# One pool for attention's tiles over the row sums, sample columns by ScalarE, adaptive weights in row tiles, bias by GpSimd

## The chip, the cores and the metric

The kernel runs on one core of a Trainium2 chip. The metric is the device time of one execution in microseconds (us). The engines are named as in the profile: PE is TensorE (matmuls; PEld is its weight load), DVE is VectorE, ACT is ScalarE, POOL is GpSimd, SP is SyncE, which here only issues transfers. Matmuls read from on-chip memory (SBUF) and write into banks of the accumulator memory (PSUM).

## The reference

One layer of a streaming encoder runs on two groups of requests that share the weights: a prompt of 1024 tokens and a sample of 32 tokens with a cache of 512 past tokens. Width 1024, eight heads of 64. Cut to what matters here:

```
ada = silu(c) @ w_ada + b_ada            # 6 vectors of 1024: shift, scale, gate, twice
h   = rms_norm(x) * (1 + scale1) + shift1
p   = h @ w_in                           # q-latent, kv-latent, rope key, q, k, v of branch B, two gates
o_A = latent attention (softmax)         # branch A
o_B: z = q k^T / 8;  sp = softplus(z) under a strict causal mask
     a = exp(log_sigmoid(z) - sum of sp over later keys);  o_B = a @ v     # branch B, stick-breaking
x   = x + gate1 * rms_norm((sigmoid(g_a) * (o_A @ w_proj_a) + sigmoid(g_b) * (o_B @ w_proj_b)) @ w_out)
x   = x + gate2 * rms_norm(conv_ffn(...))
```

Of the six vectors of ada the first two are needed before h; the other four (v = 2 to 5) are computed beside branch B's attention. All data is 32-bit floating point.

## The kernel before

Matmuls run in a reduced 32-bit format. For accuracy each operand is split into a high part (ScalarE, `hi`, L65) and a low part (VectorE, `lo`, L68), and each product is three matmuls (`mm3`, L72 to L74). Tokens are 1024 + 32 = 1056 columns; weights come in tiles of 128 by 1024.

The stages run one after the other: `stage_h` (norm, 0 to some 50 us), `stage_qkv` (projections to q, k, v), `stage_sb` (branch B's attention together with the gate projections and the rest of ada), `stage_lat` and `stage_mla` (branch A), then merge and feed-forward. The change lies in `stage_qkv` and `stage_sb` and at the border between them.

**`stage_qkv`.** The first q and k tile and a latent tile are plain products. The other ten tiles go in five pairs (`pair`) with a Strassen-like scheme: sums of quarters of h (pool "sums": T4, T3, T1, T2, two buffers each of 8448 bytes a partition, in this order of addresses) are multiplied with sums of quarters of the weights (`half`; the weights' sums are made by DVE in L585 to L590, partly in tile S1). S1 is the first 1024 columns of S0, the buffer in which the first k tile was projected. The results land in quarters of `fq` (U) as tiles of [128, 1056]. `after` then handles each finished tile: q is scaled and split, k is split, k and v are also transposed to natural order (`natural`, L466 and L472) and stored as outputs; all parts that attention needs are spilled to DRAM ("qh", "ql", "kh", "kl", "vd") by POOL's queue (L459, L478, L485). The last 32 columns of each tile, the sample's, go into one tile `sb` by a small copy on POOL (L487, L496, L504); it is stored to DRAM at the end of the stage (L665). The high part of the last two q tiles is kept in T1[0] until it is stored.

**`stage_sb`.** Four passes p, each for two heads (h = 0, 1). The order of the instructions of PE, ACT and DVE within a pass is written out by hand in `ORDER`: S is a score product, a, e, l, x, c, d, E are the steps from a score to weights, T a transpose, h and v the split of the transposed weights, V the product with the values, o and p the sum of two parts (L768, L770). Each score block has a row tile "A" (five buffers of 4096 bytes), and a score bank ("s", three) that is free again after step d (L739). "f" advances a generator, `gates().steps`: per tile m of the gate projection two adaptive steps (`ada_step`: a weight tile of 128 by 1024 from `w_ada`, eight matmuls, L216), then 24 steps of three gate matmuls. The adaptive weight tiles share the two buffers "wr" of pool W with the weight tiles of the projections. Eight adaptive steps make one vector v; its sum with the bias (L226) goes into the tile "ada" (one buffer), which the four bias transfers (L224) fill before. For v = 2 and 5 the result is stored from there (L248).

SP's queue issues the loads in the order that the planner finds: queries (L1087, six transfers of 256 KB a head), values (L1083, 512 KB), adaptive weights (L214), gate weights (L82), bias (L224). A transfer waits on the queue until its buffer is free, and all behind it wait too. The planner may move an instruction without dependencies far ahead of its place in the program, also into the hand-written order. The sample's attention (`sb_sample`) is written behind the four passes; two of its instructions stand early in the profile: the memset of QZ (L965) and the loads of cached values (L974).

**Memory.** There is a left and a right stack. On the left, above the constants and pool W, lie `fq` and the pool "qkv"; on the right, below the tiles of h, lies "sums". At the border, `att_pools` allocates the pool "att" on the left, where `fq` and "qkv" were: rows A, the transposed weights PTh and PTl, o, nat, big, QZ. `stage_sb` allocates the pool "sb" on the right over "sums": V, KL, Q and KH of both heads, reset, ptd, ada. A new tile waits for the readers of those old tiles that lay at its addresses.

Of the kernel before, what the change touches and what calls it, by code (L numbers as in the profile page):

```python
# [8 lines left out]
F32 = mybir.dt.float32  # L9
# [8 lines left out]
P = 128  # L18
D = 1024
# [25 lines left out]
class K:  # L45
# [8 lines left out]

    BUFS = {"A": 5, "Q": 3, "big": 3, "o": 2, "QZ": 1, "t": 5, "mh": 4, "ml": 4, "dh": 3, "dl": 3, "ada": 1, "G": 1, "Gs": 1, "xs": 1, "jk": 1, "s": 3, "pv": 1, "tr": 2, "mm": 2, "KSm": 1, "VSm": 1, "ObH": 1, "ObL": 1, "sg": 2}

# [149 lines left out]
    def ada_step(self, n, pool, tp, late):  # L206
# [4 lines left out]
        for i, (v, k) in enumerate(self.ada_todo[:n]):  # L211
            w = self.tl(pool, [P, D], F32, "wr")
            with self.tc.issue_after(self.begun):
                nc.sync.dma_start(w, a["w_ada"][0, k * P : (k + 1) * P, v * D : (v + 1) * D])  # L214
            for j in range(4):
                nc.tensor.matmul(ps[32 * j : 32 * j + 32, :256], self.cT[:, k], w[:, j * 256 : j * 256 + 256],  # L216
                                 start=i == 0, stop=i == n - 1)
            if i < n - 1:
                yield
        if self.ada_todo[0][1] == 0:  # L220
            self.acc = self.tl(tp, [P, 256], F32, "ada")
            for j in range(4):
                c = v * D + j * 256
                nc.sync.dma_start(self.acc[32 * j : 32 * j + 32], a["b_ada"][0, c : c + 256].partition_broadcast(32))  # L224
        acc = self.acc
# [199 lines left out]
    def stage_qkv(self):  # L425
# [35 lines left out]
        def natural(u, p, name, t0):  # L461
# [17 lines left out]
            if name == "v":  # L479
# [6 lines left out]
                else:  # L486
                    nc.gpsimd.tensor_copy(self.vsb[:, p * P : p * P + P], st[:r, :P])  # L487

        def after(kind, p, u):
# [3 lines left out]
            if kind == "q":  # L493
                QH = sg() if p == 1 else flat(T1[0])[:, TP * (p - 2) : TP * (p - 1)]
                self.hi(QH, x, 0.125)
                nc.gpsimd.tensor_scalar(self.qsb[:, p], u[:, TP:T], 0.125, None, ALU.mult)  # L496
                spill("qh", p, QH)
                stt(low, x, 0.125, fl(QH), ALU.mult, ALU.subtract)
                spill("ql", p, low)
                return  # L500
            if kind == "k":
                KH = sg()
                self.hi(KH, x)
                nc.gpsimd.tensor_copy(self.ksb[:, p], u[:, TP:T])  # L504
                spill("kh", p, KH)
# [239 lines left out]
    def sums(self, V, out, tiles):  # L745
# [3 lines left out]
        def do(k, x, h, u):  # L749
# [14 lines left out]
            else:  # L764
# [4 lines left out]
                else:  # L769
                    nc.vector.tensor_tensor(res[n][r], pv[n][r, :256], res[n][r], ALU.add)  # L770
                    out(res[n], r, slice(u * 256, u * 256 + 256))
# [188 lines left out]
    def sb_sample(self, b):  # L960
# [3 lines left out]
        QZ = self.tl(self.sm2, [P, 4, 64], F32, "QZ")  # L964
        nc.vector.memset(QZ, 0.0)  # L965
        for h in range(2):
# [3 lines left out]
        ck = self.tl(self.At, [P, TP], F32, "A")  # L970
        nc.sync.dma_start(ck.rearrange("p (t c) -> p t c", t=4),
                          a["cache_sb_k"][0, 0, :, hs].rearrange("(t p) h d -> p t (h d)", p=P))
        cv = self.tl(self.At, [P, BIG], F32, "big")
        nc.sync.dma_start(cv[:, :TP].rearrange("p (t c) -> p t c", t=4),  # L974
                          a["cache_sb_v"][0, 0, :, hs].rearrange("(t p) h d -> p t (h d)", p=P))
# [79 lines left out]

    def att_pools(self):
        nc = self.nc
        self.sm2 = self.At = self.tc.alloc_tile_pool(name="att", bufs=2, reuse_waits="tile")
        for g, w, n in (("o", 256, 2), ("big", BIG, 3), ("QZ", 256, 1), ("nat", 512, 2)):
            for _ in range(n):  # L1060
                self.tl(self.At, [P, w], F32, g)
        self.obd, self.oad = ([self.dr.tile([P, T], F32, name=f"{n}{k}") for k in range(4)] for n in ("ob", "oa"))
# [11 lines left out]
    def stage_sb(self):  # L1074
        nc = self.nc
        S = self.Sp = self.tc.alloc_tile_pool(name="sb", bufs=1, side="right", reuse_waits="tile")
        self.KLz, Q, KH, V = [None] * 2, [None] * 2, [None] * 2, [None] * 2
        t = lambda n: self.tl(S, [P, TP], F32R, n)

        def values(p, h):  # L1080
            if p:
                V[h] = t(f"V{h}")
            nc.sync.dma_start(V[h].bitcast(F32).rearrange("r (t d) -> r t d", t=8), self.vd[p][:, :, h])  # L1083

# [15 lines left out]
        first(1)  # L1100
        self.reset = S.tile([P, 512], BF16, name="reset")
        nc.vector.memset(self.reset, 1.0)
        nc.vector.tensor_scalar(self.reset[:, 383:511], self.idt, -1.0, 1.0, ALU.mult, ALU.add)
        self.diagonals(S)
        first(0)

# [10 lines left out]
        for p in range(4):  # L1117
# [3 lines left out]
            with self.tc.manual_schedule(engines={E.PE, E.Activation, E.DVE}):  # L1121
                self.sb_attend(score, lambda b, h: V[h][:, b * P : b * P + P], self.store(self.obd[p]), fill, then)
        self.in_w.append(self.next_w.pop(0))
        x = self.tl(self.At, [P, TP], F32, "A")
        self.sample_views(x)
# [3 lines left out]
        self.sample_rest = self.sb_sample(1)  # L1129
        self.Sp.release()  # L1130

# [1368 lines left out]
    def run(self, upto=99):  # L2500
        self.consts()
        self.stage_h()
        self.stage_qkv()
        self.att_pools()
        self.stage_sb()
# [60 lines left out]
```

## Time and profile before

| | us |
|---|---|
| median of 3 runs | 1715.2 (1713.25 to 1717.47) |
| the profiled execution | 1714.1 |
| its span | 1712.3 |
| PE busy | 1663.3 (97%) |
| DVE busy | 1274.1 (74%) |
| ACT busy | 991.4 (58%) |
| POOL busy | 297.3 (17%) |
| mean granted clock of PE | 0.99 of full |

The span runs from the first to the last instruction of the profiled execution. Busy times are sums over the span; matmuls are pipelined and their ends are modelled, so a busy PE may still be slow: the granted clock says how fast. An idle time before an instruction carries the name of what ended it; "issue" means that the profile shows no releaser. A transfer's "landing" is the time from its issue to its last byte. Where a row stands for several instructions (x2), its duration runs from the start of the first to the end of the last.

### The profile page before, as it was taken

What the parts mean: (1) busy time and instruction counts of PE and PEld (TensorE: products, weight loads), DVE (VectorE), ACT (ScalarE), POOL (GpSimd) and SP (SyncE); (2) the same over time, 40 slices, a digit from 0 to 9 for tenths busy, and PEclk for the clock granted to TensorE, in tenths of its full rate; (3) what the DMA queues carried; (4) which work ended last, traced back from release to release, by engine and by line L of the source; (5) the groups of instructions that cost most, each with busy time, mean ns of one, the idle gap of its engine ahead of it and who ended that gap; (6) DMA issues with size and microseconds to landing.
All of it is one profiled execution on the core that took longest, in us unless ns stands there. A gap on an engine that the chain in (4) does not pass through costs nothing. (4 is left out here: it accounts for less than half of the span.)

```text
span 1712.3 us, 30291 instructions
## 1 busy us (share of the span) xinstructions
PE 1663.3 (97%) x11646; PEld 1517.1 (89%) x11646; DVE 1274.1 (74%) x2129; ACT 991.4 (58%) x1934; POOL 297.3 (17%) x564
## 2 busy tenths in 40 slices
PE   5999799999999999999999999999999999999997
PEld 3999798998999899988889789999999999977886
DVE  4765496979794588877776779887787787788456
ACT  4544386978784577777773476544444444544442
POOL 3213211111111131111100121221121121110013
PEclk9999899999999999999999999999999999999999
DMA  9335875555633331222174531423333333697643
GB/s 329 100 120 188 277 200 170 161 164 164 175 112 93 118 97 53 65 65 71 58 275 149 182 123 54 151 93 130 130 99 133 132 102 131 233 338 240 224 141 120
DMA packets 185984, 255.19 MB, mean 149 GB/s; under 512 B 14703, under 2 KB 125569, under 8 KB 185841
## 3 DMA queue, kind: packets, MB, share of 16 engines
q1 hardware_dynamic: 165712, 194.63, 36.6%
q0 software_dynamic: 19904, 58.56, 9.7%
q8 instruction: 91, 1.49, 0.4%
q14 instruction: 53, 0.43, 0.1%
q10 hardware_dynamic: 224, 0.09, 0.0%
HBM read 187.86 MB, written 64.57 MB: 147 GB/s over the span
## 5 line engine op out<-in xcount | busy, mean ns | idle before, releaser
L65 ACT ACTIVATE wh<-wr 128x1024 fp32r<-128x1024 f32 (+5 forms) x163 | 132.1, 820 | 224.9 <-PE s L2019 78.6
L68 DVE TENSOR_TENSOR wl<-wr,wh 128x1024 fp32r<-128x1024 f32 (+5 forms) x163 | 151.3, 936 | 84.8 <-ACT wh L65 84.7
L72 PE MATMUL mm<-hh,wh 128*128 128x352 f32 x456 | 155.8, 342 | 0.0
L73 PE MATMUL mm<-hl,wh 128*128 128x352 f32 x456 | 151.1, 331 | 0.4 <-DVE hl L312 0.4
L74 PE MATMUL mm<-hh,wl 128*128 128x352 f32 x456 | 150.5, 330 | 0.0
L2018 PE MATMUL mm<-T,wh 128*128 128x256 f32 (+1 forms) x376 | 108.7, 289 | 2.6 <-ACT q L592 2.6
L2020 PE MATMUL mm<-T,wl 128*128 128x256 f32 (+1 forms) x376 | 107.6, 287 | 0.3 <-DVE wl L68 0.2
L2019 PE MATMUL mm<-T,wh 128*128 128x256 f32 (+1 forms) x376 | 107.3, 286 | 0.0
L2018 PE MATMUL s<-T,wh 128*128 128x256 f32 (+1 forms) x348 | 99.4, 286 | 0.0
L2020 PE MATMUL s<-T,wl 128*128 128x256 f32 (+1 forms) x348 | 99.2, 285 | 0.0
L2019 PE MATMUL s<-T,wh 128*128 128x256 f32 (+1 forms) x348 | 99.1, 285 | 0.0
L68 DVE TENSOR_TENSOR wl<-S,wh 128x1024 fp32r<-128x1024 f32 (+1 forms) x55 | 59.2, 1078 | 47.4 <-ACT wh L65 47.1
L72 PEld LDWEIGHTS mm<-hh,wh 128*128 128x128 f32 x456 | 87.8, 193 | 7.2 <-ACT o L768 3.3
L73 PEld LDWEIGHTS mm<-hl,wh 128*128 128x128 f32 x456 | 88.0, 193 | 2.7 <-DVE hl L312 0.9
L2159 DVE SCALAR_TENSOR_TENSOR u<-u,c,u 128x1058 f32<-128x1058 f32 x68 | 87.0, 1316 | 2.0 <-ACT u L2156 0.7
L74 PEld LDWEIGHTS mm<-hh,wl 128*128 128x128 f32 x456 | 88.0, 193 | 0.4 <-issue 0.3
L782 PE MATMUL tr<-c,A 128*128 128x128 f32 x576 | 84.1, 275 | 1.2 <-ACT A L741 0.6
L65 ACT ACTIVATE wh<-S 128x1024 fp32r<-128x1024 f32 (+1 forms) x55 | 51.8, 943 | 55.1 <-PE s L2019 13.4
L2018 PE MATMUL tr<-T,wh 128*128 128x272 f32 (+1 forms) x272 | 77.7, 286 | 0.0
L2020 PE MATMUL tr<-T,wl 128*128 128x272 f32 (+1 forms) x272 | 77.6, 285 | 0.1
L2019 PE MATMUL tr<-T,wh 128*128 128x272 f32 (+1 forms) x272 | 77.3, 284 | 0.0
L2018 PEld LDWEIGHTS mm<-T,wh 128*128 128x128 f32 x376 | 71.2, 189 | 4.1 <-ACT q L592 2.8
(754 smaller groups left out, 5785.7 us busy)
## 6 DMA issues: line engine op xcount, KB each, us to landing
wr<-in_w_ada_dram SPq DMA_DIRECT2D x48, 512.0 KB, 5.8
wr<-in_w_up_dram SPq DMA_DIRECT2D x44, 512.0 KB, 4.0
dr<-in_w_down_dram SPq DMA_DIRECT2D x43, 512.0 KB, 5.9
wr<-in_w_in_dram SPq DMA_DIRECT2D x33, 512.0 KB, 4.8
wr<-gdn SPq DMA_DIRECT2D x30, 512.0 KB, 4.9
gdn<-u POOLq DMA_DIRECT2D x23, 512.0 KB, 5.3
gd<-nat POOLq DMA_DIRECT2D x48, 176.0 KB, 2.9
t<-gd SPq DMA_DIRECT2D x16, 528.0 KB, 5.8
```

The lines of the kernel that those rows point to most:

```text
L65: self.nc.scalar.activation(out, in_, AF.Identity, scale=scale)
L68: return self.nc.vector.tensor_tensor(out, full, hi.bitcast(F32), ALU.subtract)
L72: m(ps, lh, rh, start=start, stop=False)
L73: m(ps, lh, rl, start=False, stop=False)
L74: self.pe = m(ps, ll, rh, start=False, stop=stop).ins
L782: self.nc.tensor.transpose(tr[:, (2 * s + q) * P : (2 * s + q + 1) * P], at[q][:, b * P : b * P + P], self.idt)
L2018: m(ps[:, :n], w[0][:, k], x[0][:, k, c], start=first and k == 0, stop=False, skip_group_check=True)
L2019: m(ps[:, :n], w[0][:, k], x[1][:, k, c], start=False, stop=False, skip_group_check=True)
L2020: i = m(ps[:, :n], w[1][:, k], x[0][:, k, c], start=False, stop=k == 3, skip_group_check=True)
L2159: nc.vector.scalar_tensor_tensor(y, u[:, w : w + YW], self.cvT[:, w, cc : cc + 1], y, ALU.mult, ALU.add)
```

## The change

- The tiles of branch B's attention (PTh, PTl, o, nat, and the five rows A) move from the left pool into the right pool "sb", which is now 74752 bytes and lies over "sums" and a little below it. By the order of allocation the rows A lie over the end of T3 and over T1, head 0's tiles over the end of T1 and T2, head 1's over T4 and T3, o and nat over T4[0], PTh and PTl below. The left pool "att" is allocated only behind the four passes, for the sample and branch A. `att_pools` becomes `att_rows` (the DRAM tiles alone).
- The high part of the last two q tiles is kept in T4[0], no longer in T1[0].
- The sample's columns are copied by ScalarE; for v straight from the PSUM bank.
- The first two adaptive weight tiles go into two of the rows A (`ada_first`), not into "wr".
- "ada" has two buffers, and the bias is loaded by POOL's queue.
- QZ's memset may only come behind the last sum of the passes (L770), and the loads of cached keys and values only behind the last load of values (L1083).

```diff
--- before.py
+++ after.py
@@ -52,7 +52,7 @@
         self.n += 1
         return f"{s}_{self.n}"
 
-    BUFS = {"A": 5, "Q": 3, "big": 3, "o": 2, "QZ": 1, "t": 5, "mh": 4, "ml": 4, "dh": 3, "dl": 3, "ada": 1, "G": 1, "Gs": 1, "xs": 1, "jk": 1, "s": 3, "pv": 1, "tr": 2, "mm": 2, "KSm": 1, "VSm": 1, "ObH": 1, "ObL": 1, "sg": 2}
+    BUFS = {"A": 5, "Q": 3, "big": 3, "o": 2, "QZ": 1, "t": 5, "mh": 4, "ml": 4, "dh": 3, "dl": 3, "ada": 2, "G": 1, "Gs": 1, "xs": 1, "jk": 1, "s": 3, "pv": 1, "tr": 2, "mm": 2, "KSm": 1, "VSm": 1, "ObH": 1, "ObL": 1, "sg": 2}
 
     def tl(self, pool, shape, dt=F32, tag=None, bufs=None):
         return pool.tile(shape, dt, tag=tag, name=self.nm(tag or "t"), bufs=bufs or self.BUFS.get(tag))
@@ -209,7 +209,7 @@
         nc, a = self.nc, self.a
         ps = self.bank("mm")
         for i, (v, k) in enumerate(self.ada_todo[:n]):
-            w = self.tl(pool, [P, D], F32, "wr")
+            w = self.ada_first.pop(0) if self.ada_first else self.tl(pool, [P, D], F32, "wr")
             with self.tc.issue_after(self.begun):
                 nc.sync.dma_start(w, a["w_ada"][0, k * P : (k + 1) * P, v * D : (v + 1) * D])
             for j in range(4):
@@ -221,7 +221,7 @@
             self.acc = self.tl(tp, [P, 256], F32, "ada")
             for j in range(4):
                 c = v * D + j * 256
-                nc.sync.dma_start(self.acc[32 * j : 32 * j + 32], a["b_ada"][0, c : c + 256].partition_broadcast(32))
+                nc.gpsimd.dma_start(self.acc[32 * j : 32 * j + 32], a["b_ada"][0, c : c + 256].partition_broadcast(32))
         acc = self.acc
         late.append(lambda: nc.vector.tensor_tensor(acc, acc, ps[:, :256], ALU.add))
         del self.ada_todo[:n]
@@ -484,16 +484,16 @@
                     add(V[:, :, :, 64:128], sv, fl(V[:, :, :, 0:64]), ALU.subtract)
                     nc.gpsimd.dma_start(self.vd[p][:, t0 : t0 + 4], fl(V))
                 else:
-                    nc.gpsimd.tensor_copy(self.vsb[:, p * P : p * P + P], st[:r, :P])
+                    nc.scalar.copy(self.vsb[:, p * P : p * P + P], tr[:r, :P])
 
         def after(kind, p, u):
 
             x = u[:, :TP]
             low = x.bitcast(F32R)
             if kind == "q":
-                QH = sg() if p == 1 else flat(T1[0])[:, TP * (p - 2) : TP * (p - 1)]
+                QH = sg() if p == 1 else flat(T4[0])[:, TP * (p - 2) : TP * (p - 1)]
                 self.hi(QH, x, 0.125)
-                nc.gpsimd.tensor_scalar(self.qsb[:, p], u[:, TP:T], 0.125, None, ALU.mult)
+                nc.scalar.mul(self.qsb[:, p], u[:, TP:T], 0.125)
                 spill("qh", p, QH)
                 stt(low, x, 0.125, fl(QH), ALU.mult, ALU.subtract)
                 spill("ql", p, low)
@@ -501,7 +501,7 @@
             if kind == "k":
                 KH = sg()
                 self.hi(KH, x)
-                nc.gpsimd.tensor_copy(self.ksb[:, p], u[:, TP:T])
+                nc.scalar.copy(self.ksb[:, p], u[:, TP:T])
                 spill("kh", p, KH)
             for t0 in (0, 4, 8):
                 natural(u, p, kind, t0)
@@ -767,7 +767,7 @@
                     res[n] = self.tl(self.At, [P, 256], F32, "o")
                     nc.scalar.copy(res[n][r], pv[n][q, :256])
                 else:
-                    nc.vector.tensor_tensor(res[n][r], pv[n][r, :256], res[n][r], ALU.add)
+                    self.sum_ins = nc.vector.tensor_tensor(res[n][r], pv[n][r, :256], res[n][r], ALU.add).ins
                     out(res[n], r, slice(u * 256, u * 256 + 256))
 
         return do
@@ -962,16 +962,19 @@
         nc, a = self.nc, self.a
         os = self.osb
         QZ = self.tl(self.sm2, [P, 4, 64], F32, "QZ")
-        nc.vector.memset(QZ, 0.0)
+        with self.tc.issue_after(self.sum_ins):
+            nc.vector.memset(QZ, 0.0)
         for h in range(2):
             r, pc = slice(64 * h, 64 * h + 64), slice(2 * b, 2 * b + 2)
             nc.vector.tensor_copy(QZ[r, pc, 32 * h : 32 * h + 32], self.qsb[r, pc])
         hs = slice(4 * b, 4 * b + 4)
         ck = self.tl(self.At, [P, TP], F32, "A")
-        nc.sync.dma_start(ck.rearrange("p (t c) -> p t c", t=4),
+        with self.tc.issue_after(self.fetched):
+            nc.sync.dma_start(ck.rearrange("p (t c) -> p t c", t=4),
                           a["cache_sb_k"][0, 0, :, hs].rearrange("(t p) h d -> p t (h d)", p=P))
         cv = self.tl(self.At, [P, BIG], F32, "big")
-        nc.sync.dma_start(cv[:, :TP].rearrange("p (t c) -> p t c", t=4),
+        with self.tc.issue_after(self.fetched):
+            nc.sync.dma_start(cv[:, :TP].rearrange("p (t c) -> p t c", t=4),
                           a["cache_sb_v"][0, 0, :, hs].rearrange("(t p) h d -> p t (h d)", p=P))
         mm = [self.tl(self.At, [P, TP], F32, "A") for _ in range(2)]
         for pp in range(2):
@@ -1053,12 +1056,7 @@
 
         return do
 
-    def att_pools(self):
-        nc = self.nc
-        self.sm2 = self.At = self.tc.alloc_tile_pool(name="att", bufs=2, reuse_waits="tile")
-        for g, w, n in (("o", 256, 2), ("big", BIG, 3), ("QZ", 256, 1), ("nat", 512, 2)):
-            for _ in range(n):
-                self.tl(self.At, [P, w], F32, g)
+    def att_rows(self):
         self.obd, self.oad = ([self.dr.tile([P, T], F32, name=f"{n}{k}") for k in range(4)] for n in ("ob", "oa"))
         self.gd = self.dr.tile([16, P, T], F32, name="gd")
         self.pbd = self.dr.tile([8, P, T], F32, name="pbd")
@@ -1073,14 +1071,18 @@
 
     def stage_sb(self):
         nc = self.nc
-        S = self.Sp = self.tc.alloc_tile_pool(name="sb", bufs=1, side="right", reuse_waits="tile")
+        self.att_rows()
+        S = self.Sp = self.At = self.tc.alloc_tile_pool(name="sb", bufs=2, side="right", reuse_waits="tile")
+        for g, w, n in (("PTh", 512, 2), ("PTl", 512, 2), ("o", 256, 2), ("nat", 512, 2)):
+            for _ in range(n):
+                self.tl(S, [P, w], F32R if g[0] == "P" else F32, g)
         self.KLz, Q, KH, V = [None] * 2, [None] * 2, [None] * 2, [None] * 2
-        t = lambda n: self.tl(S, [P, TP], F32R, n)
+        t = lambda n: self.tl(S, [P, TP], F32R, n, 1)
 
         def values(p, h):
             if p:
                 V[h] = t(f"V{h}")
-            nc.sync.dma_start(V[h].bitcast(F32).rearrange("r (t d) -> r t d", t=8), self.vd[p][:, :, h])
+            self.fetched = nc.sync.dma_start(V[h].bitcast(F32).rearrange("r (t d) -> r t d", t=8), self.vd[p][:, :, h]).ins
 
         def queries(p, h):
             r, o = slice(64 * h, 64 * h + 64), slice(64 - 64 * h, 128 - 64 * h)
@@ -1098,10 +1100,13 @@
             V[h], self.KLz[h], Q[h], KH[h] = t(f"V{h}"), t(f"KL{h}"), t(f"Q{h}"), t(f"KH{h}")
 
         first(1)
-        self.reset = S.tile([P, 512], BF16, name="reset")
+        self.reset = S.tile([P, 512], BF16, name="reset", bufs=1)
         nc.vector.memset(self.reset, 1.0)
         nc.vector.tensor_scalar(self.reset[:, 383:511], self.idt, -1.0, 1.0, ALU.mult, ALU.add)
         self.diagonals(S)
+        self.ada_first = [self.tl(S, [P, D], F32, "A") for _ in range(2)]
+        for _ in range(3):
+            self.tl(S, [P, TP], F32, "A")
         first(0)
 
         self.begun = queries(0, 0)
@@ -1121,13 +1126,14 @@
             with self.tc.manual_schedule(engines={E.PE, E.Activation, E.DVE}):
                 self.sb_attend(score, lambda b, h: V[h][:, b * P : b * P + P], self.store(self.obd[p]), fill, then)
         self.in_w.append(self.next_w.pop(0))
+        S.release()
+        self.sm2 = self.At = self.tc.alloc_tile_pool(name="att", bufs=2, reuse_waits="tile")
         x = self.tl(self.At, [P, TP], F32, "A")
         self.sample_views(x)
         self.osb = x[:, 768:896].rearrange("p (k t) -> p k t", k=4)
         for r, c in self.SB:
             nc.sync.dma_start(x[r, c], self.sbd[r, c])
         self.sample_rest = self.sb_sample(1)
-        self.Sp.release()
 
 
     def lat_sums(self, sq):
@@ -2501,7 +2507,6 @@
         self.consts()
         self.stage_h()
         self.stage_qkv()
-        self.att_pools()
         self.stage_sb()
         self.stage_lat()
         self.stage_mla()
```

## The prediction

> **What bounds the kernel now.** I read the page first: its first part (busy time of each engine) and the rows for PE and DMA of its second (forty equal slices).
>
> ```profile
> span 1712.3 us, 30291 instructions
> PE 1663.3 (97%) x11646; PEld 1517.1 (89%) x11646; DVE 1274.1 (74%) x2129; ACT 991.4 (58%) x1934; POOL 297.3 (17%) x564
> PE   5999799999999999999999999999999999999997
> DMA  9335875555633331222174531423333333697643
> ```
>
> TensorE sets the end: 1712.3 − 1663.3 = 49 us of the span are without a matmul. A gain can come only from those 49 us and from matmuls at a low granted clock. The change touches slices 2 to 13 of 42.8 us each, and the fifth (171 to 214 us) is the poor one: PE at 7 tenths, DMA at 8. So I took busy time by stretch next, around every place in those slices where PE stood. The columns are stretch, length, busy us (instructions) of PE, PEld, DVE, ACT and POOL, then clock, DMA share, GB/s.
>
> ```profile
> 88.00:92.00 4.00, 2.72 (x18) 2.72 (x19) 4.00 (x6) 2.09 (x4) 0.01 (x1) 0.84 0.34 135
> 92.00:96.00 4.00, 4.00 (x26) 4.00 (x26) 4.00 (x6) 2.20 (x5) 0.00 (x0) 0.73 0.52 131
> 195.00:200.00 5.00, 1.73 (x17) 0.95 (x14) 3.74 (x6) 1.31 (x2) 3.11 (x8) 0.99 1.02 409
> 210.00:215.00 5.00, 3.44 (x12) 3.24 (x13) 4.49 (x10) 4.05 (x10) 0.00 (x0) 0.52 1.02 213
> 215.00:220.00 5.00, 5.00 (x29) 5.00 (x28) 3.02 (x8) 3.81 (x9) 0.86 (x2) 0.80 1.06 266
> 288.00:292.00 4.00, 2.28 (x24) 1.14 (x23) 2.42 (x7) 3.55 (x12) 0.55 (x1) 1.00 1.00 326
> 292.00:296.00 4.00, 4.00 (x17) 3.92 (x16) 2.13 (x4) 0.38 (x1) 0.00 (x0) 0.57 0.62 186
> ```
>
> Three places, each an idle PE followed by a low clock: near 87 us (start of the paired projections), 196 to 217 us (from projections to attention), 289 to 296 us (attention's second pass). The change meets all three. Below, rows of the timeline give start, us, engine and line; a bracket gives the idle time before and what ended it.
>
> **1. Sample's columns to ScalarE (L487, L496, L504).** Eleven small copies leave POOL.
>
> ```profile
> 69.02 8.07 POOL L504 COPY sb<-S 128x32 f32<-128x32 f32 x1 [5.78 <-ACT S L649]
> L504 POOL COPY sb<-fq x3: 209/209/211, 128.5 to 150.1; 128x32 f32<-128x32 f32 x3
> 79.08 0.55 POOL L459 DMA_DIRECT2D kl<-S  x1
> DMA to landing us min/median/max: 4.5/4.5/4.5
> 83.62 0.69 DVE L585 TENSOR_TENSOR S<-wr 128x512 f32<-128x512 f32 x1 [6.60 <-issue]
> 89.28 0.39 PE L2018 MATMUL mm<-T,wh 128*128 128x256 f32 x1 [2.58 <-ACT q L592]
> L641 ACT ACTIVATE sb<-mm x1: 198/198/198, 62.4 to 62.4; 128x32 f32<-128x32 f32 x1
> ```
>
> The first of L504 took 8.07 us where the other three took 0.21, and POOL's queue stood behind it until 77.1: the key store kl<-S went out at 79.08, 2.0 us after the copy, and landed 4.5 us later (its landing row), at 83.6. That is when DVE's L585 starts, which overwrites the S that the store still reads. So the 6.60 us of DVE, called "issue", are this store, and DVE was free at 83.62 − 6.60 = 77.0. Without the copy POOL sends its stores as their inputs come; the same chain with 0.2 in place of 8.07 puts kl 7.9 earlier, at 71.2, if its input is there, and a store that waits for its input some 2 us more: 73.7, landing at 78.2. L585 and the ScalarE copies behind it (L592) then come 83.6 − 78.2 = 5.4 us earlier, more than the 2.58 that PE waited for L592, so that wait goes. The low clock behind it cost 4 × (1 − 0.73) = 1.1 in 92 to 96 and up to 4 × (1 − 0.84) = 0.6 before, together some 1.6. Gain 2.6 + 1.6 = 4.2. Late next is PE's own queue: its stretch from 92 on is full.
>
> ScalarE takes the eleven at 0.2 us (L641's row, the same shape): 2.2 us, on an engine busy 2.09 of 4 us here, each behind a ScalarE operation that needs the same input. Bounds: 0, and 2.2 if each lay on PE's path. I take 0.4, nearer to the covered end.
>
> **2. The border to attention.**
>
> ```profile
> 197.90 0.64 PE L216 MATMUL mm<-wr,cT 128*32 128x256 f32 x8 [1.81 <-ACT T L65]
> 201.21 1.08 PE L216 MATMUL mm<-wr,cT 128*32 128x256 f32 x8 [2.67 <-DMA wr<-in_w_ada_dram]
> 206.49 0.46 PE L74 MATMUL mm<-hh,wl 128*128 128x352 f32 x1
> 211.56 0.76 PE L1112 MATMUL s<-KH,Q 128*128 128x512 f32 x1 [4.61 <-DVE A L739]
> 199.67 0.29 DVE L1103 TENSOR_SCALAR reset<-c 128x128 bf16<-128x128 f32 x1
> 209.28 0.27 DVE L965 MEMSET QZ<- 128x256 f32 x1 [9.32 <-DMA ql<-fq]
> 196.78 1.06 ACT L65 ACTIVATE T<-fq 128x1024 fp32r<-128x1024 f32 x1 [1.18 <-DVE fq L576]
> 201.12 0.28 ACT L721 ACTIVATE A<-s 128x128 f32<-128x128 f32 x1 [3.29 <-DMA out_dram<-nat]
> 186.63 7.74 SPq L214 DMA_DIRECT2D wr<-in_w_ada_dram  x2
> ```
>
> PE's 4.61 waits for DVE's L739, which frees the score bank; L739 is late because DVE's queue stood 9.32 us at the memset of QZ. That tile is for the sample's attention, 300 us later; it lies where the projections' buffers were, and their store ql<-fq landed at 209. ScalarE's first L721 waits for such a store in the same way. In the changed kernel the row tiles A lie over T1 and the end of T3, which are read out before the projections end, and the memset is tied behind the last L770. So L721 can run behind the last split of the queries (196.78 + 1.06 = 197.8), five more short ScalarE operations bring DVE's L727 to about 200, where L1103 ends, and L739 frees the bank 211.56 − 209.28 = 2.3 us later, at 202.3. The next step is late instead: the two adaptive loads. They now go out together (before: 186.63 and 7.74 later), but one behind the other on SP's queue, with the DMA at a share of 1.02. So I leave 1.81 and 2.67 as they are; the other bound is that both go, 4.5. PE then comes to its next score at 206.49 + 0.46 = 206.95, and the 4.61 are gone. So is the low clock behind them: (215 − 211.56) × (1 − 0.52) + 5 × (1 − 0.80) = 1.65 + 1.0 = 2.6. I take 2.5. Gain 7.1.
>
> A rule beside that row: the Trainium skill, "TensorE: Matmul & The Clock Gate", Part 1, puts the warm-up at about 3.4 us at half clock, an estimate of 1.7 us lost for each stall. By the rule the term would be 4.6 + 1.7 = 6.3; the rows show more lost here, and the rows decide.
>
> The queries' high part moves from T1 to T4: its two stores (L459) now hold V1 back and no longer Q1. V1 belongs to the second pair of heads, which starts later. Priced 0; what covers it are the first pair's blocks.
>
> **3. Bias by POOL, two buffers.**
>
> ```profile
> SPq L224 <- DMA gtd<-ada: 6.4, 1, 6.4
> 284.12 0.56 SPq L1083 DMA_DIRECT2D V<-vd  x1
> 285.29 0.35 SPq L214 DMA_DIRECT2D wr<-in_w_ada_dram  x1
> 290.90 0.64 PE L216 MATMUL mm<-wr,cT 128*32 128x256 f32 x8 [1.72 <-DMA wr<-in_w_ada_dram]
> 288.62 0.55 POOL L1044 DMA_DIRECT2D gd<-nat  x1 [3.31 <-ACT A L721]
> 299.37 0.54 POOL L1044 DMA_DIRECT2D gd<-nat  x1 [10.20 <-ACT nat L1043]
> 369.99 0.54 POOL L1044 DMA_DIRECT2D gd<-nat  x1 [3.32 <-ACT A L721]
> 377.51 0.54 POOL L1044 DMA_DIRECT2D gd<-nat  x1 [6.98 <-ACT nat L1043]
> 443.58 0.55 SPq L1083 DMA_DIRECT2D V<-vd  x1
> 446.32 0.35 SPq L214 DMA_DIRECT2D wr<-in_w_ada_dram  x1
> ```
>
> SP stood 6.4 us until the one bias buffer was stored. So V left at 284.12, 1.2 us before the adaptive load of 285.29; that load landed at 290.9, and PE wanted it at 290.90 − 1.72 = 289.2. In a pass where nothing held SP, V leaves 2.7 us ahead of that load (443.58, 446.32). The price of the stall with its low clock: from 288.62 to 299.37 lie 10.75 us, between the same two stores one pass later 377.51 − 369.99 = 7.52. That is 3.2; I take 3.0, since a shorter wait may stay. POOL gets sixteen issues of 0.54 us, 8.6 us on an engine 17% busy: 0. Its queue carries only stores here; what waits for the bias is DVE's sum of it, which the order of work places some steps after the issue.
>
> **4. The sample's loads move.**
>
> ```profile
> 224.60 0.38 SPq L974 DMA_DIRECT2D big<-in_cache_sb_v_dram  x1
> DMA to landing us min/median/max: 5.0/5.0/5.0
> DMA to landing us min/median/max: 4.1/4.1/4.1
> ```
>
> Cached keys (L971) and values (L974) may now issue only behind the last V load, 443.58, and the buffers of the keys are free by then. Up to three loads of 512 KB can come in before the adaptive load of 446.32, which has no slack: it lands 4.1 us later (second landing row), at 450.4, when PE wants it. Bounds: 0 if they go behind it, as the value load of before went behind an adaptive load in the first pass; and 3 × 5.0 (the first landing row, of the value loads) = 15 us of stall with 2.5 of low clock, 17.5. I take 0, by the nearest row, 224.60.
>
> **Sum.** 4.2 − 0.4 + 7.1 + 3.0 = 13.9. The profiled execution took 1714.1 (its span 1712.3 and 1.8 around it), 1.1 under the median of 1715.2. 1714.1 − 13.9 = 1700.2; against the median 1701.3.
>
> **The rivals.**
> A. kl<-S is late through traffic and not through POOL, and part 1 gives nothing: 1715.2 − 9.7 = 1705.5. Against it: the store's issue itself is late, right behind the copy.
> B. The bias move gives nothing, since the load of 285.29 is slow through traffic: 1701.3 + 3.0 = 1704.3. For it: a DMA share of 1.00 from 288 to 292. Against it: what held V was a semaphore. The Trainium skill, "DMA: Bandwidth & Descriptors", section "Issuing engines are not separate DMA queues", says that another issuing engine saves only issue time, since all share the same 16 engines; that rule makes B.
> C. Part 4 at a middle price. Three loads at 1.3 us (512 KB at the 409 GB/s of 195 to 200) are 3.9, with 2 of low clock 5.9: 1707.2. At 3.3 each (what the second adaptive load took behind the first, 201.2 − 197.9) 9.9 + 2.5 = 12.4: 1713.7, no change.
> D. The memset goes, but another row tile or store holds DVE or ScalarE about as long, and part 2 gives half or nothing: 1704.9 to 1708.4.
> E. Slower: part 4 at its dear end, 17.5 against 13.9: 1718.8. It decides from 13.9 us on, 3.8 of stall a load with the clock. For it: no slack at 446.32. Against it: all three would have to land one after another.
>
> **How the numbers follow.** Forecast 0.48, A 0.10, B 0.10, C 0.19 (0.12 cheap, 0.07 dear), D 0.07, E 0.06. The forecast's own range runs from 1701.3 − 4.5 = 1696.8 (both adaptive waits go) to 1703.1 (ScalarE at 2.2). The whole range, 1696 to 1709, takes in A, B, D and the cheap C. A measurement here tells about 0.3%, 5.1 us, from no change: faster 0.48 + 0.10 + 0.10 + 0.12 + 0.07 = 0.87, same 0.07, slower 0.06.
>
> **What would show it.** Part 1: no POOL copy of 8 us, DVE's L585 before 80 us, PE without a pause at 87. Part 2: the first L727 near 196 (part 1 moves it by 4), no wait of PE for L739, full clock from about 203. Part 3: no wait of PE over 0.5 us for the adaptive load that answers to 285.29. Part 4: the order on SP's queue around the last V load, and whether PE waits behind it. I am wrong if that wait is over 3 us, or if PE waits at the border for something new, such as a row tile that a late store still reads.

## The result, and the profile after

The changed kernel takes 1716.53 us (median of 12 runs, 1711.95 to 1721.04) against 1716.07 for the kernel before (12 runs in the same set): a ratio of 1.0006, with a 95% interval of 0.9994 to 1.0017. That is no change. The prediction of 1701.3 us, and its whole range, are missed.

The profiled execution of the changed kernel took 1719.25 us (span 1716.4), 2.7 above its median. These are the rows of its page that answer to those shown of before:

```profile
span 1716.4 us, 30275 instructions
PE 1663.4 (97%) x11646; PEld 1516.1 (88%) x11646; DVE 1272.2 (74%) x2129; ACT 994.1 (58%) x1945; POOL 297.0 (17%) x569
PE   5999799999998999999999999999999999999997
DMA  9345855565533331222174531423333333697643
```

The fifth slice is still the poor one, and the thirteenth (515 to 558 us), at 9 before, is now at 8. So there are two places to look at. Busy time by stretch (same columns as in the prediction):

```profile
60.00:100.00 40.00, 39.97 (x289) 39.65 (x288) 34.63 (x43) 21.01 (x38) 4.91 (x8) 1.00 0.38 120
180.00:220.00 40.00, 30.01 (x195) 27.61 (x195) 20.51 (x38) 19.13 (x46) 14.28 (x27) 0.83 0.85 302
210.00:215.00 5.00, 3.08 (x11) 3.08 (x12) 3.16 (x6) 0.96 (x2) 1.63 (x4) 0.69 0.50 179
260.00:300.00 40.00, 39.82 (x283) 37.34 (x282) 29.59 (x51) 28.38 (x63) 9.63 (x18) 1.00 0.58 170
500.00:560.00 60.00, 55.54 (x365) 51.22 (x364) 26.87 (x55) 27.62 (x59) 6.55 (x13) 0.97 0.36 101
```

The stop near 87 us is gone (39.97 busy of 40), and the second pass is full (39.82). The border is as empty as before, and 500 to 560 lost some 4 us (PE was busy 59.72 of these 60 before). The timeline names the holders at the border; the first row is DVE's L585 of the projections, at 78.78 where it was at 83.62:

```profile
78.78 0.69 DVE L585 TENSOR_TENSOR S<-wr 128x512 f32<-128x512 f32 x1 [0.53 <-DVE T L68]
194.68 0.53 ACT L721 ACTIVATE A<-s 128x128 f32<-128x128 f32 x2
197.78 1.08 PE L216 MATMUL mm<-A,cT 128*32 128x256 f32 x8 [4.87 <-ACT A L725]
200.23 1.08 PE L216 MATMUL mm<-A,cT 128*32 128x256 f32 x8 [1.37 <-DMA A<-in_w_ada_dram]
198.30 0.37 POOL L1069 MEMSET ptd<- 128x128 f32 x2
200.27 0.50 POOL L224 DMA_DIRECT2D ada<-in_b_ada_dram  x1 [1.60 <-DMA qh<-T]
202.73 0.99 POOL L224 DMA_DIRECT2D ada<-in_b_ada_dram  x2 [1.96 <-DMA vd<-sg]
206.33 0.50 POOL L224 DMA_DIRECT2D ada<-in_b_ada_dram  x1 [2.62 <-DMA qh<-T]
210.98 0.42 DVE L226 TENSOR_TENSOR ada<-ada,mm 128x256 f32<-128x256 f32 x1 [10.58 <-DMA ada<-in_b_ada_dram]
211.32 0.55 DVE L739 TENSOR_TENSOR A<-s,A 128x384 f32<-128x384 f32 x1
211.92 0.64 PE L1117 MATMUL s<-KH,Q 128*128 128x320 f32 x1 [3.75 <-DVE A L739]
```

ScalarE's first L721 no longer waits for a store, and QZ's memset is gone from here. But the four bias transfers on POOL's queue go out at 200.27, 202.73 and 206.33, each only when an earlier store of that queue has landed. DVE's sum of the bias (L226) stands 10.58 us for the last of them, L739 stands behind it, and TensorE stands 3.75 us for L739. The clock of 0.69 from 210 to 215 follows.

The second place is the sample's part, behind the four passes:

```profile
505.55 18.51 SPq L82 DMA_DIRECT2D wr<-in_w_in_dram  x4
524.11 1.15 SPq L1135 DMA_DIRECT2D A<-sbd  x2
525.31 0.42 SPq L973 DMA_DIRECT2D A<-in_cache_sb_k_dram  x1
525.78 1.05 SPq L977 DMA_DIRECT2D big<-in_cache_sb_v_dram  x2
531.29 1.06 PE L984 MATMUL tr<-c,A 128*128 128x128 f32 x8 [2.14 <-DMA A<-in_cache_sb_k_dram]
545.46 1.10 PE L954 MATMUL pv<-A,big 128*128 128x64 f32 x8 [1.26 <-ACT A L941]
530.00:540.00 10.00, 8.47 (x45) 7.14 (x46) 4.23 (x11) 4.28 (x12) 0.00 (x0) 0.83 0.50 151
```

The sample's columns, keys and values, which I had feared too early, come too late. On SP's queue they stand behind four weight loads that wait 18.51 us for their buffers.

Three marks measure each stretch finer than a time of the whole: ScalarE's first copy L768 (end of the border), its last one (end of the passes), and the weight split L65 next after the sample's part. Their rows in the profile before and then in that after:

```profile
218.59 0.37 ACT L768 COPY o<-pv 64x256 f32<-64x256 f32 x1 [0.27 <-PE pv L796]
522.45 0.36 ACT L768 COPY o<-pv 64x256 f32<-64x256 f32 x1 [2.28 <-PE pv L796]
559.68 1.06 ACT L65 ACTIVATE wh<-wr 128x1024 fp32r<-128x1024 f32 x1 [2.21 <-PE s L73]
```

```profile
215.47 0.37 ACT L768 COPY o<-pv 64x256 f32<-64x256 f32 x1 [2.18 <-PE pv L796]
516.24 0.36 ACT L768 COPY o<-pv 64x256 f32<-64x256 f32 x1 [2.28 <-PE pv L796]
559.70 1.06 ACT L65 ACTIVATE wh<-wr 128x1024 fp32r<-128x1024 f32 x1 [2.38 <-PE s L73]
```

At the last copy the changed kernel is 522.45 − 516.24 = 6.2 us ahead in these two profiles; at the third mark nothing is left. The same marks for all kernels, with the experiments below (us; the last column is the span less the third mark):

| kernel | first L768 | passes | sample's part | rest |
|---|---|---|---|---|
| before / again | 218.59 / 216.33 | 303.9 / 302.7 | 37.2 / 37.3 | 1152.6 / 1154.9 |
| after / again | 215.47 / 213.18 | 300.8 / 305.3 | 43.5 / 42.8 | 1156.7 / 1154.6 |
| e1 bias on SP | 207.29 | 303.6 | 43.0 | 1154.3 |
| e2 sample first | 215.41 | 300.5 | 38.2 | 1156.7 |
| e5 both / again | 208.16 / 207.24 | 302.2 / 302.8 | 38.2 / 38.2 | 1157.1 / 1153.4 |
| e3 ScalarE copies | 214.23 | 301.8 | 37.3 | 1154.2 |
| e4 bias on POOL | 214.19 | 301.1 | 37.3 | 1161.4 |
| e6 late memset | 217.12 | 303.2 | 37.3 | 1154.7 |
| e7 no move | 216.51 | 301.4 | 37.3 | 1155.7 |
| e8 gates first | 206.87 | 301.3 | 38.2 | 1154.5 |
| e10 one buffer | 207.03 | 306.3 | 38.2 | 1155.2 |

Two profiles of one kernel differ by up to 2.3 us at the first mark, 4.5 in the passes and 3.7 in the rest, but by no more than 0.7 in the sample's part. So a difference of the passes under some 5 us is not read from this table. The rest of e4, 1161.4, lies 4 us above the next; that profile took 1715.74 us, 3.4 above its kernel's median, and the cause stays open.

### The profile page after: what moved, and what is told of

Same layout as the page of the kernel before. It is cut to its first block, busy times and chain, and to the rows that moved or that the text cites. A ratio compares the mean times of both kernels' runs of the same rounds, so it can differ in the third digit from the quotient of the medians.

```text
span 1716.4 us, 30275 instructions
## 1 busy us (share of the span) xinstructions
PE 1663.4 (97%) x11646; PEld 1516.1 (88%) x11646; DVE 1272.2 (74%) x2129; ACT 994.1 (58%) x1945; POOL 297.0 (17%) x569
## 5 line engine op out<-in xcount | busy, mean ns | idle before, releaser
L65 ACT ACTIVATE wh<-wr 128x1024 fp32r<-128x1024 f32 (+5 forms) x163 | 132.1, 820 | 222.8 <-PE s L2025 74.5
L65 ACT ACTIVATE wh<-S 128x1024 fp32r<-128x1024 f32 (+1 forms) x55 | 51.8, 943 | 50.9 <-PE s L2025 13.4
L68 DVE TENSOR_TENSOR PTl<-tr,PTh 128x512 fp32r<-128x512 f32 x96 | 64.6, 683 | 12.8 <-ACT PTh L65 12.5
```

What stands on the lines that cost most here:

```text
L65: self.nc.scalar.activation(out, in_, AF.Identity, scale=scale)
L68: return self.nc.vector.tensor_tensor(out, full, hi.bitcast(F32), ALU.subtract)
```

## The experiments

**The two losses, each repaired and then both.** In the first kernel the bias goes back to SP's queue, with its two buffers kept:

```diff
-                nc.gpsimd.dma_start(self.acc[32 * j : 32 * j + 32], ...
+                nc.sync.dma_start(self.acc[32 * j : 32 * j + 32], ...
```

> The changed kernel with the bias (line 224) put back on SP's queue, its two buffers kept. Theory A (the bias on POOL's queue is what the first border waits for: DVE's sum on line 226 waited 10.58 us there, TensorE 3.75 us behind it and a low clock until 215): the 10.58 us wait goes, the first V matmul (line 796) moves from 214.38 to about 210.5, the second pass keeps its gain because the second buffer, not the queue, removed the 6.4 us stall, and the time falls by 3 to 5 us against the changed kernel (about 1712 against 1716). Rival B (the border is bound by DMA traffic, and the bias only waits in another queue): line 226 still waits until about 211 and the time stays within 1 us. Rival C (the lead is lost at the end of attention in any case): line 796 comes earlier but the mark at 560.8 (line 68 after the passes) and the time do not move.

Measured: 1710.0 us against 1714.71 for before, ratio 0.9973 (0.9962 to 0.9983). The border of this kernel, on SP, DVE and PE:

```profile
184.88 1.53 SPq L224 DMA_DIRECT2D ada<-in_b_ada_dram  x2
187.83 2.07 SPq L224 DMA_DIRECT2D ada<-in_b_ada_dram  x2
199.18 0.42 DVE L226 TENSOR_TENSOR ada<-ada,mm 128x256 f32<-128x256 f32 x1
195.74 1.08 PE L216 MATMUL mm<-A,cT 128*32 128x256 f32 x8 [3.87 <-DMA A<-in_w_ada_dram]
198.04 1.08 PE L216 MATMUL mm<-A,cT 128*32 128x256 f32 x8 [1.22 <-DMA A<-in_w_ada_dram]
```

The bias leaves 15 us earlier, L226 waits for nothing, and the first mark falls from 215.47 to 207.29. At the border theory A holds and B falls. C falls too, since the third mark comes 5.8 us earlier; but the sample's part costs 43.0 here as well, so the second loss is a separate one. One clause of theory A fell: the second pass does not keep its gain. SP stands 6.9 us for the store gtd<-ada again, with two buffers, and the gain in the second pass is gone (the table under "What is left").

In the second kernel the next weight loads may issue only behind the sample's:

```diff
-    def wload(self, parts):
+    def wload(self, parts, after=None):
...
+            with self.tc.issue_after(after) if after else self.ctx.__class__(): nc.sync.dma_start(...)
...
-        raw = self.wload([(0, 1024, self.a["w_in"] ..., 8)])
+        raw = self.wload([(0, 1024, self.a["w_in"] ..., 8)], self.held)
...
+            cvl = nc.sync.dma_start(cv[:, :TP] ...); self.held = self.held or cvl.ins
```

> The changed kernel with the w_in loads of the stage behind attention issued only after the sample's first four loads (x, keys, values), so that these stand ahead of three w_in loads in SP's queue instead of behind them. Theory A (the 6.2 us lead at the end of the passes is lost because these loads are issued at 524 instead of 501 to 506): they are issued at about 506, TensorE's waits of 2.14 us (line 984) and 1.26 us (line 954) and the low clock from 530 to 550 go, and the time falls by 4 to 7 us against the changed kernel (about 1711). Rival B (the lead is lost for another reason, such as the order of the second w_in tile's matmuls, or the w_in loads now come late instead): the waits move to other lines and the mark at 560.8 stays within 1.5 us.

Measured: 1711.39 us against 1714.71, ratio 0.9982 (0.9973 to 0.9991). SP's queue and the stretch from 530 on in this kernel:

```profile
505.60 1.09 SPq L1135 DMA_DIRECT2D A<-sbd  x2
506.73 0.48 SPq L973 DMA_DIRECT2D A<-in_cache_sb_k_dram  x1
508.44 10.58 SPq L82 DMA_DIRECT2D wr<-in_w_in_dram  x2
530.00:540.00 10.00, 10.00 (x66) 9.43 (x64) 5.35 (x9) 5.31 (x11) 0.00 (x0) 1.00 0.38 107
```

The loads leave 18 us earlier, PE is full at full clock, and the sample's part takes 38.2 where it took 43.5. Theory A holds. Of the microsecond that is left against the 37.3 of before, 0.67 is a wait of TensorE for ScalarE (L993 for L985, at 526.53), which the kernel before does not have; the rest stays open.

> The changed kernel with both edits: bias on SP's queue with two buffers, and the sample's loads ahead of the next stage's w_in loads. If the two losses are separate and each is what Theory A says, the gains add: 7 to 12 us under the changed kernel (about 1707), which is faster than both kernels. If one of them hides the other, the gain is that of the larger alone, 4 to 6 us.

Measured: 1704.76 us against 1714.71, ratio 0.9941 (0.9928 to 0.9954). Repeated in another set:

> The changed kernel with both repairs once more, beside the run with one buffer: the time that this is to be compared with, on the same chip. If the first result holds, the ratio to before is 0.993 to 0.995 again.

Measured: 1704.34 us against 1715.74, ratio 0.9943 (0.9927 to 0.9960). The gains add, within the intervals: against the changed kernel's 1.0006, e1 is 0.0033 lower, e2 0.0024 and both together 0.0065. This kernel beats the one before by 10 us.

**The parts one by one, on the kernel before.**

```diff
-                    nc.gpsimd.tensor_copy(self.vsb[:, p * P : p * P + P], st[:r, :P])
+                    nc.scalar.copy(self.vsb[:, p * P : p * P + P], tr[:r, :P])
...
-                nc.gpsimd.tensor_scalar(self.qsb[:, p], u[:, TP:T], 0.125, None, ALU.mult)
+                nc.scalar.mul(self.qsb[:, p], u[:, TP:T], 0.125)
...
-                nc.gpsimd.tensor_copy(self.ksb[:, p], u[:, TP:T])
+                nc.scalar.copy(self.ksb[:, p], u[:, TP:T])
```

> The kernel before with the sample's copies on ScalarE alone (part 1 of the prediction, nothing else). By the prediction's own sum: 3.8 us faster than before (about 1712). By the theory formed from the trace after (the adaptive weights land at 197.8 and 200.2 whether the sums end 3.2 us earlier or not, because the DMA engines are full from 180 to 205): TensorE's pause of 2.58 us near 87 goes, the first score moves from 195.0 to about 191.8, but the gate matmuls still start near 201 to 202, and the time falls by 1 us at most.

Measured: 1710.75 us against 1714.71, ratio 0.9982 (0.9973 to 0.9992), 3 to 4 us faster. POOL's store and DVE's L585 in this kernel:

```profile
74.83 0.55 POOL L459 DMA_DIRECT2D kl<-S  x1
78.56 0.69 DVE L585 TENSOR_TENSOR S<-wr 128x512 f32<-128x512 f32 x1 [0.55 <-DVE T L68]
```

The store landed 3.7 us after its issue, at 78.5, and L585 started at 78.56, as the prediction's chain has it. The prediction's sum held; the theory that I had formed from the trace after, that the border swallows this gain, fell.

```diff
-        nc.vector.memset(QZ, 0.0)
+        with self.tc.issue_after(self.sum_ins): nc.vector.memset(QZ, 0.0)
```

> The kernel before with the memset of QZ held back behind the last sum of attention (the part of the prediction's part 2 that frees DVE at the border), nothing else. By the prediction: DVE's hold of 9.32 us goes, TensorE's wait of 4.61 us on line 1112 and the low clock of 2.5 us behind it go, 7.1 us faster than before (about 1707.6). Rival (the row maxima of the second block wait for something else that lands near 205 to 208 as well, the bias or the third adaptive load): 3 us or less.

Measured: 1714.19 us against 1715.08, ratio 0.9996 (0.9985 to 1.0006): nothing that can be told from no change. ScalarE's and DVE's rows at the border of this kernel say why:

```profile
201.46 0.28 ACT L721 ACTIVATE A<-s 128x128 f32<-128x128 f32 x1 [3.70 <-DMA out_dram<-nat]
204.34 0.38 ACT L721 ACTIVATE A<-s 128x256 f32<-128x256 f32 x1 [2.60 <-DMA vd<-sg]
209.65 0.49 ACT L721 ACTIVATE A<-s 128x384 f32<-128x384 f32 x1 [3.92 <-DMA sbd<-sb]
205.45 0.73 DVE L727 SCALAR_TENSOR_TENSOR A<-s,A 128x128 f32<-128x128 f32 x2 [5.58 <-ACT A L725]
211.34 0.56 DVE L727 SCALAR_TENSOR_TENSOR A<-s,A 128x384 f32<-128x384 f32 x1 [3.46 <-ACT A L725]
```

The memset had stood beside a second hold of the same length: three row tiles, each waiting for a store to land, the last at 209.65 (210.28 before). That hold is there in before, e3, e6 and e7, which leave the rows where they were; in the changed kernel, which moves them, it is not.

The next kernel has only the bias on POOL and the second buffer (`"ada": 2`, and `nc.gpsimd.dma_start` for the bias).

> The kernel before with the bias's loads on POOL's queue and two buffers for them (part 3 alone). By the prediction: 3.0 us faster than before (1711.7 against 1714.7), because the 6.4 us stall of SP goes and POOL's issues are priced at nothing. By Theory A (POOL's issue waits for earlier stores on its queue, so the first bias lands near 211): DVE's sum on line 226 waits at the first border too, but most of that wait lies beside the memset's hold of DVE, which ends near 207; so the border loses 0 to 4 us, the second pass still gains about 1.5, and the time lies between 1 us faster and 3 us slower than before.

Measured: 1712.39 us against 1715.08, ratio 0.9987 (0.9976 to 0.9998). In this kernel the late bias costs nothing at the border, since DVE still stands at the memset until 205.86. The same edit costs 7 us there once the memset and the rows are out of the way. In the second pass it gains 2.8 us (the table under "What is left"), so here part 3 alone gave about what was forecast.

The next has ScalarE's copies, the late memset and two bias buffers on SP, and moves no pool and no load.

> The kernel before with ScalarE's copies, the late memset and two bias buffers on SP's queue; the pools, the sample's loads and the adaptive weights' tiles stay as before. If parts 1, 2 and 3 are worth what the prediction gave them (4.2 less 0.4, 7.1 and 3.0) and the losses came only from POOL's queue and from the moved pool, this is about 1701 to 1703, at least as fast as the changed kernel with both repairs (10 us under before in the first set of runs). If the moved pool and the row tiles bring a gain of their own at the border, it is 2 us or more slower than that kernel.

Measured: 1708.43 us against 1715.08, ratio 0.9964 (0.9952 to 0.9976). The first mark is at 216.51, 8 to 9 us behind e5 (208.16 and 207.24), and ScalarE's L721 waits for the same three stores as in e6, the last until 208.09: without the pool's move the gain at the border doesn't come. The size is less sure. This profile is that of the slowest of eight runs (1712.67 us), and by the times the kernel lies some 4 us behind e5. The adaptive weights in row tiles, which e7 leaves out too, were not tested apart from the move.

**What is left.** One bias buffer instead of two in the kernel with both repairs (`"ada": 1`):

> The changed kernel with both repairs, but with one bias buffer instead of two (the bias on SP's queue as before): what is left of part 3 is undone. By the prediction SP then stands 6.4 us for the one buffer in the second pass, and the kernel is 3.0 us slower than the one with both repairs (about 1707.8 against 1704.8 when before is 1714.7). Rival: with the adaptive loads in other tiles and the passes shifted by some 10 us, nothing that TensorE needs stands behind the stall, and the two are equal within 1 us.

Measured: 1707.82 us against 1704.34 for two buffers in the same set; the ratios to before are 0.9955 (0.9942 to 0.9968) and 0.9943 (0.9927 to 0.9960). By the times alone the intervals overlap. SP and PE in the second pass show the stall and whom it holds:

```profile
269.23 2.84 SPq L224 DMA_DIRECT2D ada<-in_b_ada_dram  x4
273.52 0.39 SPq L214 DMA_DIRECT2D wr<-in_w_ada_dram  x1
280.43 1.08 PE L216 MATMUL mm<-wr,cT 128*32 128x256 f32 x8 [3.02 <-DMA wr<-in_w_ada_dram]
SPq L224 <- DMA gtd<-ada: 6.5, 3, 6.2
```

But the stall is there with two buffers as well, as e5 shows:

```profile
271.41 2.68 SPq L224 DMA_DIRECT2D ada<-in_b_ada_dram  x4
SPq L224 <- DMA gtd<-ada: 6.8, 1, 6.8
```

With two buffers the bias of the second vector leaves early, at 206 to 215 us, and at 271.41 it is the bias of the third that stands: it needs the buffer of the first, whose store has not landed. The passes as a whole (306.3 against 302.2 and 302.8) differ by no more than two profiles of one kernel do. A narrower stretch does better, the way into the second pass, from the eighth copy L768 to the ninth. First before, then after:

```profile
282.56 0.36 ACT L768 COPY o<-pv 64x256 f32<-64x256 f32 x1 [2.23 <-PE pv L796]
300.37 0.37 ACT L768 COPY o<-pv 64x256 f32<-64x256 f32 x1
```

```profile
279.64 0.36 ACT L768 COPY o<-pv 64x256 f32<-64x256 f32 x1 [2.28 <-PE pv L796]
294.36 0.37 ACT L768 COPY o<-pv 64x256 f32<-64x256 f32 x1
```

| bias | kernels | eighth to ninth L768, us |
|---|---|---|
| SP's queue, one buffer | before / again, e3, e6, e10 | 17.81 / 17.74, 16.23, 16.21, 20.13 |
| SP's queue, two buffers | e1, e5 / again, e7, e8 | 17.63, 15.76 / 16.12, 16.14, 16.03 |
| POOL's queue, two buffers | after / again, e2, e4 | 14.72 / 14.40, 14.67, 14.93 |

The four profiles with the bias on POOL's queue, where SP never stands for it, lie below all others: 17.8 − 14.6 = 3.2 us from before to after, and at least 0.8 against any kernel with the bias on SP's queue. What the second buffer alone is worth on SP's queue is not shown: e10 lies 4 us above e5 here and 3.5 in the times, but e3 and e6, with one buffer, lie at e7's value, and e1, with two, at that of before. One buffer on POOL's queue was not run.

In the next kernel four of the first gate tile's eight k steps stand ahead of the first two adaptive steps:

```diff
-                yield from self.ada_step(2, self.W, self.Sp, ada)
+                if m: yield from self.ada_step(2, self.W, self.Sp, ada)
+                else: first = self.bank("mm")
...
+                        if (m, b, k) == (0, 0, 4): yield from self.ada_step(2, self.W, self.Sp, ada, first)
```

> The changed kernel with both repairs (bias on SP, sample's loads first), and in the first gate tile four of the eight k steps (twelve matmuls of 352 columns) stand ahead of the first two adaptive steps. Theory: what TensorE still waits for at the border, 4.8 and 1.2 us on line 216, is the landing of the adaptive weights, which traffic sets (DMA share 1.03 to 1.06 from 180 to 205), so work that needs no load fills it: the twelve matmuls run inside the wait (some 2 us at full clock, up to 4 at half), and the time falls by 1.5 to 3 us against that kernel (about 1702.5 when before is 1714.7). Rival: the wait only moves, since the twelve matmuls would have found a free TensorE later anyway (within 1 us).

Measured: 1703.98 us against 1715.17, ratio 0.9940 (0.9926 to 0.9953), not told apart from e5 (0.9941 and 0.9943). The two waits ahead of L216 fell only from 4.8 us in e5 (3.53 + 1.25 and 3.28 + 1.54) to 2.40 + 1.92 = 4.3, and the first mark, 206.87, lies by the 207.03 to 208.16 of the kernels without the edit. So the theory is not shown; the rival, that the wait only moves, is nearer.

**How far profiles of the same code differ.**

> The kernel before once more, for a second profile of it: how far two profiles of the same code differ between 560 us and the end. The profile of before runs that stretch 3.4 to 4.1 us faster than the profile of the changed kernel, though the medians of the whole differ by 0.5. If that is spread between executions, this profile lies between the two, or nearer the slower one; if the changed kernel is slower there for a reason of its own, it agrees with the first profile to within 1 us.

> The changed kernel once more, for a second profile and a second set of times on the chip of this set. If the two losses found are what keeps it at no change, the same waits stand in this profile (line 226 at the border some 10 us, the sample's loads issued behind 520), and the time is again within 0.3% of before.

Measured: 1712.93 us for before (one run), and 1716.89 for after against 1715.17, ratio 1.0011 (1.0000 to 1.0021). The rest behind the third mark takes 1152.6 and 1154.9 before, 1156.7 and 1154.6 after: spread, and no effect of the change. Both losses of the changed kernel stand in its second profile too: 10.1 us of DVE at L226, the sample's columns issued at 526.31.

## Why the prediction was wrong, by its own steps

**Part 1, right.** Forecast 4.2 − 0.4 = 3.8; e3 gained 3 to 4, L585 came before 80 and PE's stop at 87 went. The store kl<-S left at 74.83, where the prediction had 73.7 (its own terms, 71.2 and some 2, make 73.2), and L585 came at 78.56 instead of 78.2. Why POOL's copy took 8.07 us was not tested; it ended at 77.1, when an unbroken run of DVE's operations ended at 77.0.

**Part 2, right in size, but its gain never arrived.** Parts 1 and 2 together were to bring 10.9 by the end of the border. With the bias repaired they bring 217.5 (mean of the two profiles of before) − 207.4 (mean of e1, e5 twice and e10) = 10.0. The two waits for adaptive weights, kept at 1.81 + 2.67 = 4.5, are 3.87 + 1.22 = 5.1 in e1. The reasoning named the rows' move and the memset together, and e6 and e7 show that the first is needed. What the step missed is that L226 stands in DVE's queue ahead of L739: "L739 frees the bank 211.56 − 209.28 = 2.3 us later, at 202.3" took for granted that the bias lies there.

**Part 3, the step that failed: "POOL gets sixteen issues of 0.54 us, 8.6 us on an engine 17% busy: 0."** It priced the engine and not the queue. The next sentence saw the queue ("Its queue carries only stores here") and did not ask whether these had landed when the first bias was due. The first marks of after (215.47, 213.18) and e2 (215.41), mean 214.7, against 207.4 give 7.3 us for it. The other half of the part, 3.0 for SP's stall, was right: 3.2 in the changed kernel and 2.8 in e4. Rival B, no gain from the move, falls. The second buffer alone, which the expectations of e1 and e10 credit with it, does not free SP's queue: with two buffers there SP still stands 6.5 to 7.0 us for the store. So the same move gained 3.2 in one place and cost 7.3 in another.

**Part 4, the second failed step: "Bounds: 0 ... and ... 17.5. I take 0, by the nearest row".** Both bounds spoke of loads that come early and collide at 446. Nothing came early: in the changed kernel the adaptive load behind the last V load left at 440.26, and TensorE waited 0.42 us for it (1.88 in the second profile). Neither bound asked what stands ahead of the sample's loads if they come late. The mean of 43.5, 42.8 and 43.0 (after twice, e1) less 37.25 is 5.9 us. Rival C's cheap case named the same 5.9, but by a mechanism that did not occur.

The sum with these terms: −10.0 − 3.2 + 7.3 + 5.9 = 0.0, against a measured ratio of 1.0006, which is +1.0 us (−1.0 to +2.9). The likeliest case was wrong because two steps were given no price at all. The range was wrong because each rival stood alone: D had a hold of DVE in the memset's place (of a row tile or a store, at up to 7.1) and C's cheap case a loss of 5.9 at part 4, and both together would have been 1701.3 + 7.1 + 5.9 = 1714.3. The sign of failure that the prediction named, TensorE waiting at the border for something new, did appear, with the bias in the place of a row tile.

## What to carry to other kernels

When a transfer is moved to another queue, read what that queue holds at the moment of its first use: what must land before it may issue, and what on the consuming engine stands behind it. When a load is tied to come later or its buffer is allocated later, price its being late as well as its being early, by what then stands ahead of it on its queue. Two holds side by side, as the memset and the row tiles here, show as one wait in the profile; removing the named one alone may be worth nothing (e6), and an edit that is free beside them (e4) may cost its full price once they are gone. When a stall has gone after a change of two things, undo each alone before crediting one: here the buffer looked like the cure, and with the bias back on SP's queue the stall was back in spite of it.

## What the hardware showed beyond that

The waits of POOL's queue follow a pattern. In the built program each transfer of POOL's waits on one of eight semaphores, in turn, and so for the transfer eight places before it. (The numbers in front count POOL's instructions; two of the ten from 80 to 90 are the memsets of ptd.)

```
80 L459 DMA qh_536<-T_514 128x1024 [waits DMASW2_49,Activation_49]
81 L485 DMA vd_552<-sg_2118 128x1024 [waits DMASW3_49,DVE_49]
...
90 L224 DMA ada_2254<-in_b_ada_dram 32x256 [waits DMASW2_49]
91 L224 DMA ada_2254<-in_b_ada_dram 32x256 [waits DMASW3_49]
```

The trace agrees by name: the first two bias issues follow the landing of qh<-T (issued at 191.57) and vd<-sg (192.38), 9 and 10 us after those two were issued, at a DMA share of 1.03. No run changed the number of these semaphores, so that they set the 7.3 us rests on these names. SP's queue has eight such semaphores too; in e1 one wait of 1.0 us for a load, KL<-kl, is named among its bias issues at the border. The Trainium skill, "DMA: Bandwidth & Descriptors", section "Issuing engines are not separate DMA queues", says that another issuing engine saves only issue time. The trace differs: the bias on POOL's queue gained 3.2 us in the second pass and cost 7.3 at the border, and both came from what else stood on the queue, not from the time to issue.

The adaptive and gate matmuls of the border ran at a granted clock of 0.50 from 200 to 205 in the changed kernel and were busy 4.77 of those 5 us, so about 2.4 us of that stretch were lost with hardly a wait of TensorE in it. The kernel before had the same clock there (0.50, busy 3.79 of 5), so this is no effect of the change:

```profile
200.00:205.00 5.00, 4.77 (x21) 3.97 (x22) 0.40 (x1) 0.00 (x0) 1.49 (x3) 0.50 1.03 401
```
